# The rest of each w_down weight: a negated rounding on ScalarE and an adding DMA inside SBUF in place of a subtraction on VectorE

## The chip, the cores and the metric

The kernel runs on one core of a Trainium2 chip. The metric is the time of one execution on the device in microseconds, the median of several runs. One execution was also recorded by the hardware profiler, and all rows below are from that one.

## The reference

Two transformer blocks over 256 tokens of width 2048, in float32. The change lies in the feed-forward part of the first block, whose hidden width is 5632:

```python
h2 = rms_norm(x, norm2_g[l])
x = x + (jax.nn.silu(h2 @ w_gate[l]) * (h2 @ w_up[l])) @ w_down[l]
```

Before it stand the first block's two attentions (`w_in`, `w_out`), after it the second block's even and odd layers. Nearly all the work is products of a [256 x K] activation with a [K x N] weight that is read once from HBM.

## The kernel before

A float32 product is made of three products in float32r, a form with a shorter mantissa. Each operand v is split in `hi`, v rounded to float32r, and `lo`, the rest v - hi, also in float32r. TensorE then makes activation hi by weight hi, activation hi by weight lo, and activation lo by weight hi (L186, L187, L188).

`linear` (L168) does one product for 512 output columns. It walks over groups of 512 rows of the weight. For each group SP fetches one tile `raw` [128, 4, 512] (1 MB, L124) from HBM; three such tiles exist. A group is two pairs of row blocks. For each pair, `split` (L153) makes `hi` [128, 2, 512] by a cast on ScalarE (L155) and `lo` by a subtraction on VectorE (L156); three `hi` and three `lo` tiles exist. TensorE then runs twelve products on the pair: two row blocks, two tiles of 128 tokens, three products each. The results gather in two PSUM tiles `acc`.

The feed-forward part (L507 to L539) loops over 11 blocks `j` of 512 hidden columns: `linear` on `w_gate` (4 groups), `linear` on `w_up` (4 groups), the gate, a transposition to `mh` and `ml`. After j = 2, 4, 6, 8 it calls `down` on two blocks and after j = 10 on three. `down` does four `linear` on `w_down`, one per 512 output columns, each over two (at the end three) groups. So `w_down` is read in four stretches of 8 groups and a last one of 12: 44 groups, 88 pairs. They are called stages here. In the last one each column block is finished by `x_done` (transposes and splits of the new stream, sums of squares).

The order on each engine is set by a scheduler when the program is built, each engine runs its instructions in that order, and each waits on semaphores for what it reads and for the tile that it writes to be free. SP's fetch of a group waits until the tile of three groups before has been read by the last of its readers.

The tiles called `u` are the work tiles of the attentions (`unit`, L102); of these 0, 1, 2, 3, 6, 7, 8 and 11 are free during the feed-forward part.

Of the kernel before, what the change touches and what calls it, by code (L numbers as in the profile page):

```python
# [18 lines left out]
P = 128  # L19
# [5 lines left out]

# constants that depend on shapes alone, by column of one [128, *] array
CU, CR, CIND, CID, CMASK, COMASK, CGE, CLE, CGT, COROPE, CEND = 0, 128, 256, 258, 386, 514, 642, 770, 898, 1026, 1282


def _constants():  # L30
    c = np.zeros((P, CEND), np.float32)
    s, t = np.arange(P)[:, None], np.arange(P)[None, :]
    same = (s // 64) == (t // 64)
    c[:, CU:CU + P] = (same & (s <= t)) / 16.0
    c[:, CR:CR + P] = (same & (s > t)) / 16.0
    c[:, CIND:CIND + 2] = (np.arange(P)[:, None] // 64 == np.arange(2)[None, :]) / 16.0
    c[:, CID:CID + P] = s == t
    c[:, CMASK:CMASK + P] = same & (s <= t)
    c[:, COMASK:COMASK + P] = np.where(s >= t, 0.0, NEG)
    c[:, CGE:CGE + P] = s >= t  # L40
    c[:, CLE:CLE + P] = s <= t
    c[:, CGT:CGT + P] = s > t

    def angles(d):
        f = np.float32
        inv = f(1.0) / (f(10000.0) ** (np.arange(0, d, 2, dtype=f) / f(d)))
        ang = np.arange(S, dtype=f)[:, None] * inv[None, :]
        cos, sin = np.cos(ang).astype(f), np.sin(ang).astype(f)
        return cos.reshape(2, P, d // 2).transpose(1, 0, 2), sin.reshape(2, P, d // 2).transpose(1, 0, 2)

    co, so = angles(64)
    c[:, COROPE:COROPE + 128] = np.concatenate([co, co], 2).reshape(P, 128)
    c[:, COROPE + 128:COROPE + 256] = np.concatenate([-so, so], 2).reshape(P, 128)

    # even layer: rope tables and the decay of the retention, keys on partitions
    ce, se = angles(256)
    gam = np.zeros((P, 4, S), np.float64)
    diff = np.arange(S)[None, :] - np.arange(P)[:, None]
    for h in range(4):
        gam[:, h] = np.where(diff >= 0, (1.0 - 2.0 ** (-5.0 - h)) ** np.maximum(diff, 0), 0.0)  # L60
    ev = np.concatenate([ce.reshape(P, 256), se.reshape(P, 256), gam.reshape(P, 1024)], 1).astype(np.float32)

    # relative bias: bucket of each distance, and the log of how many patterns hold it
    x = np.arange(384)
    d = 255 - x
    dd = np.clip(d, 0, None)
    big = 16 + (np.log(np.maximum(dd, 1) / 16) / np.log(2048 / 16) * 16).astype(np.int64)
    bucket = np.where(dd < 16, dd, np.minimum(big, 31))
    oneh = (bucket[None, :] == np.arange(32)[:, None]).astype(np.float32)
    cnt = (d >= 0) * ((d <= 128) * 1 + (d % 4 == 0) * 1 + (d % 16 == 0) * 1)  # L70
    lnc = np.where(cnt > 0, np.log(np.maximum(cnt, 1)), NEG).astype(np.float32)
    rel = np.zeros((32, 768), np.float32)
    rel[:, :384] = oneh
    rel[:, 384:] = lnc[None, :]
    return {"c_main": c, "c_even": ev, "c_rel": rel}
# [3 lines left out]
def model(ctx, tc, a, out):  # L79
# [31 lines left out]

# [1 line left out]
    cm = cst.tile([P, CEND], F32, tag="cm", name="cm")  # L113
# [37 lines left out]

# [1 line left out]
    def split(hi, lo, src, scale=None):  # L153
# [10 lines left out]

    # small products of an attention, dealt out among the large ones
    side = deque()

    def linear(w, c0, n, groups, got=(), fine=False):  # L168
        accs = [ps_acc.tile([P, 512], F32, tag="acc", name=nm("acc")) for _ in range(2)]
        for gi, ((xh, xl), kg) in enumerate(groups):  # L170
            raw = got[gi] if gi < len(got) else fetch(w, kg, c0, n)
            for k in range(4):
                k2 = k % 2
                if k2 == 0:
                    hi = hl_p.tile([P, 2, 512], F32R, tag="hi", name=nm("hi"))
                    lo = hl_p.tile([P, 2, 512], F32R, tag="lo", name=nm("lo"))
                    if fine and gi == 0:
                        for j in range(2):
                            split(hi[:, j, :n], lo[:, j, :n], raw[:, k + j, :n])
                    else:  # L180
                        split(hi[:, :, :n], lo[:, :, :n], raw[:, k:k + 2, :n])
                for t in range(2):
                    o = accs[t][:, :n]
                    st, en = gi == 0 and k == 0, gi == len(groups) - 1 and k == 3
                    sl = slice(t * P, (t + 1) * P)
                    T.matmul(o, xh[:, k, sl], hi[:, k2, :n], start=st, stop=False)  # L186
                    T.matmul(o, xh[:, k, sl], lo[:, k2, :n], start=False, stop=False)  # L187
                    T.matmul(o, xl[:, k, sl], hi[:, k2, :n], start=False, stop=en)  # L188
                    if side:
                        side.popleft()()  # L190
        return accs

# [1 line left out]
    def new_stream():  # L194
# [40 lines left out]
    def head_scale(accs_t, nh, r, r2, t):  # L235
        """per token and head: r * (r^2 * mean of squares + eps)^-0.5"""
        dh = 512 // nh
# [11 lines left out]
    def finish_head(po, gate, g_off, rowf, chunk, mixT, scales):  # L249
        """o [tok, 256] of one head in po [128, 2, 256]: RMS over it, the gate, transposed and split"""  # L250
        s, q = small([2], "fs"), small([2], "fq")
# [22 lines left out]
    def silu_gate(dst, acc, rh_t):  # L274
        """(1 + tanh(z/2)) * acc, z = 2 rh acc: silu(z) is this by rh"""
        A.activation(dst, acc, AF.Tanh, scale=rh_t)  # L276
        V.scalar_tensor_tensor(dst, dst, 1.0, acc, ALU.add, ALU.mult)  # L277

    def transpose_rows(src, dst, scale=None):
        """src(t) [128 tok, 4 x 128] -> dst [128, 4, 256]"""  # L280
        for j in range(2):
# [10 lines left out]

    # ================= first block: mixers =================
    st = new_stream()
# [12 lines left out]

    # r and the gate's low rank part
    got = first
# [79 lines left out]

    # relative bias of the dilated heads by distance  # L390
    relr = sm.tile([P, 384], F32, tag="Lx", name="relr", bufs=4)
    pt = ps_w.tile([P, 512], F32, tag="w", name=nm("at"))
    T.matmul(pt[:8, :384], rb[0:32, :], rel[0:32, 0:384], start=True, stop=True)
    V.tensor_tensor(relr[:8, :], pt[:8, :384], rel[0:8, 384:768], ALU.add)
    # laid down once a row; a row pitch read one short turns it into a Toeplitz table
    reld = dr.tile([8, 384], F32, name="reld", tag="reld")
# [47 lines left out]

    # dilated attention: the three patterns are one softmax, a distance counted as often as patterns hold it
    Tb = []
# [59 lines left out]

    # ================= first block: feed forward =================  # L507
    w_gate, w_up, w_down = a["w_gate"][0], a["w_up"][0], a["w_down"][0]
# [6 lines left out]
    def down(bs, last):  # L515
        for b in range(4):
            x_add(b, linear(w_down, b * 512, 512, [(acts[j], j) for j in bs]))
            if last:
# [23 lines left out]

    # ================= second block, even layer =================
    ev_w_in, ev_w_out = a["ev_w_in_2"][0], a["ev_w_out_2"][0]
# [58 lines left out]

    # gated convolution, half a width at a time; channels on partitions for the taps
    rc = small([2], "rc")
# [48 lines left out]

    # ================= second block, odd layer =================
    od_w_in, od_w_out = a["od_w_in_2"][0], a["od_w_out_2"][0]
    mixT = [pair(mt_p, "m") for _ in range(4)]
    # rope tables with the norm weights in them: x * ra + swapped(x) * rb
    ra = cst.tile([P, 2, 2, 64], F32, tag="ra", name="ra")
# [9 lines left out]
    def rope_odd(dst, acc, nh, w, t, scale):  # L669
        """acc [128, nh*64] -> dst, roped and scaled per head"""  # L670
        n = nh * 64
# [15 lines left out]
    for t in range(2):  # L687
        q = head_scale(accs[t], 8, r, r2, t)
        rope_odd(krow[:, t], accs[t], 4, 1, t, q)
        A.activation(vo[:, t], accs[t][:, 256:], AF.Copy, scale=r[:, t:t + 1])  # L690
    # keys of a group twice, the dead half zero: a pair of query heads in one product
    kz = [unit(2 + i, [2, 2, S], F32R) for i in range(2)]
# [23 lines left out]
    def att_scores(c):  # L716
        """queries of a tile against their 128 keys: of tile 1 the keys past a query's own place are the first
        tile's, so one square holds the whole window"""
        g, t, u = c["g"], c["t"], c["u"]
# [60 lines left out]
    def att_values(c):  # L780
        """values still, probabilities moving: two heads side by side, transposed as the output product wants them"""
        g, t, u = c["g"], c["t"], c["u"]
# [105 lines left out]
```

## Time and profile before

| | |
|---|---|
| Median of three runs | 1939.45 us (1939.33 to 1939.72) |
| Span of the profiled execution | 1937.7 us |
| What the median has beyond that span | 1.75 us |
| TensorE busy in the span | 1925.6 us, 99% |
| VectorE, ScalarE, GpSimd busy | 1090.8, 900.2, 193.5 us |
| Moved by the DMA engines | 356.16 MB, mean 184 GB/s |

Engines are named PE (TensorE's products), PEld (its weight loads), DVE (VectorE), ACT (ScalarE), POOL (GpSimd), SP (the queue that fetches). A name with q behind it (SPq, POOLq) is the engine's sequencer. Busy time counts records of instructions. Records of products overlap by some 0.16 us (one is 0.39 us long and they start every 0.23 us), so a busy PE says that it never ran dry, not that it is at its peak. The DMA share is the mean over the 16 DMA engines of the time that their packets took; packets overlap, so it can pass 1.

### The profile page before, as it was taken

What the parts mean: (1) busy time and instruction counts of PE and PEld (TensorE: products, weight loads), DVE (VectorE), ACT (ScalarE), POOL (GpSimd) and SP (SyncE); (2) the same over time, 40 slices, a digit from 0 to 9 for tenths busy, and PEclk for the clock granted to TensorE, in tenths of its full rate; (3) what the DMA queues carried; (4) which work ended last, traced back from release to release, by engine and by line L of the source; (5) the groups of instructions that cost most, each with busy time, mean ns of one, the idle gap of its engine ahead of it and who ended that gap; (6) DMA issues with size and microseconds to landing.
All of it is one profiled execution on the core that took longest, in us unless ns stands there. A gap on an engine that the chain in (4) does not pass through costs nothing.

```text
span 1937.7 us, 22600 instructions
## 1 busy us (share of the span) xinstructions
PE 1925.6 (99%) x8928; PEld 1591.1 (82%) x8928; DVE 1090.8 (56%) x1287; ACT 900.2 (46%) x1239; POOL 193.5 (10%) x314
## 2 busy tenths in 40 slices
PE   8999999999999999999999999999999999999999
PEld 8877888888888888888888888888888888788787
DVE  5445555565555555555555555555555666677654
ACT  6544544454444434434444544444444355566543
POOL 2000221100000000000000001010000003754100
PEclk9999999999999999999999999999999999999999
DMA  8564555555555555555555555555556555443364
GB/s 286 194 211 157 178 183 171 190 175 193 182 190 196 195 186 185 194 195 191 184 192 194 187 183 178 172 189 169 186 192 196 184 185 193 159 143 137 131 206 141
DMA packets 181050, 356.16 MB, mean 184 GB/s; under 512 B 6072, under 2 KB 14288, under 8 KB 180816
## 3 DMA queue, kind: packets, MB, share of 16 engines
q1 hardware_dynamic: 179888, 351.03, 54.4%
q0 software_dynamic: 912, 3.64, 0.7%
q8 instruction: 70, 1.15, 0.2%
q14 instruction: 36, 0.29, 0.0%
q10 hardware_dynamic: 144, 0.05, 0.0%
HBM read 352.59 MB, written 3.68 MB: 184 GB/s over the span
## 4 chain that ended last, share of the span: by engine, by line
PE 98%; POOL 1%; DVE 0%; DMA 0%; ACT 0%; SPq 0%; issue 0%; ACTq 0%
PE acc L186 30%; PE acc L187 30%; PE acc L188 30%; PE at L787 1%; PE tr L204 1%; PE tr L286 1%; PE tr L535 0%; PE tr L768 0%; DMA xT<-in_x_t_dram 0%; PE at L735 0%; PE at L737 0%; PE at L736 0%; PE at L592 0%; PE at L441 0%; PE at L436 0%; PE at L429 0%
## 5 line engine op out<-in xcount | busy, mean ns | idle before, releaser
L156 DVE TENSOR_TENSOR lo<-raw,hi 128x1024 fp32r<-128x1024 f32 (+3 forms) x666 | 816.1, 1227 | 721.0 <-ACT hi L155 719.4
L155 ACT CAST hi<-raw 128x1024 fp32r<-128x1024 f32 (+3 forms) x666 | 692.4, 1040 | 865.6 <-PE acc L188 854.5
L187 PE MATMUL acc<-lo,xh 128*128 128x512 f32 (+3 forms) x1920 | 748.7, 390 | 0.4 <-DVE lo L156 0.4
L188 PE MATMUL acc<-hi,xl 128*128 128x512 f32 (+3 forms) x1920 | 742.9, 387 | 0.0
L186 PE MATMUL acc<-hi,xh 128*128 128x512 f32 (+3 forms) x1920 | 685.4, 389 | 6.3 <-ACT hi L155 6.3
L186 PEld LDWEIGHTS acc<-hi,xh 128*128 128x128 f32 x1920 | 359.9, 188 | 80.4 <-ACT hi L155 6.7
L187 PEld LDWEIGHTS acc<-lo,xh 128*128 128x128 f32 x1920 | 361.1, 188 | 72.5 <-issue 1.7
L188 PEld LDWEIGHTS acc<-hi,xl 128*128 128x128 f32 x1920 | 361.2, 188 | 71.3 <-issue 2.1
L187 PE MATMUL acc<-lo,mh 128*128 128x512 f32 x736 | 288.4, 392 | 0.0
L188 PE MATMUL acc<-hi,ml 128*128 128x512 f32 x736 | 286.7, 390 | 0.0
L186 PE MATMUL acc<-hi,mh 128*128 128x512 f32 x736 | 264.9, 392 | 0.0
L188 PEld LDWEIGHTS acc<-hi,ml 128*128 128x128 f32 x736 | 138.2, 188 | 28.1
L187 PEld LDWEIGHTS acc<-lo,mh 128*128 128x128 f32 x736 | 138.2, 188 | 28.1
L186 PEld LDWEIGHTS acc<-hi,mh 128*128 128x128 f32 x736 | 137.8, 188 | 28.2
L219 POOL TENSOR_SCALAR st_s<-st_s 128x2 f32<-128x2 f32 x4 | 0.8, 192 | 985.9 <-DVE st_s L218 985.9
L233 DVE TENSOR_TENSOR x<-x,acc 128x512 f32<-128x512 f32 x80 | 51.3, 680 | 5.6 <-PE acc L188 5.6
L276 ACT ACTIVATE u<-acc,st_rh 128x512 f32<-128x512 f32 (+3 forms) x46 | 29.2, 653 | 17.5 <-PE acc L188 16.7
L277 DVE SCALAR_TENSOR_TENSOR u<-u,acc 128x512 f32<-128x512 f32 (+3 forms) x46 | 28.8, 639 | 9.5 <-ACT u L276 9.5
L158 ACT ACTIVATE xh<-tr,gc 128x256 fp32r<-128x256 f32 x48 | 20.1, 471 | 20.7 <-PE tr L204 19.8
L755 ACT ACTIVATE Lx<-Lx,omx 128x128 f32<-128x128 f32 x64 | 24.9, 392 | 8.8 <-POOL omx L752 7.4
L159 DVE SCALAR_TENSOR_TENSOR xl<-tr,gc,xh 128x256 fp32r<-128x256 f32 x48 | 21.0, 478 | 11.5 <-ACT xh L158 11.5
L150 POOL TENSOR_TENSOR hq<-hs,nhalf 128x8 f32<-128x8 f32 (+1 forms) x18 | 25.9, 1438 | 0.8
(202 smaller groups left out, 854.1 us busy)
## 6 DMA issues: line engine op xcount, KB each, us to landing
raw<-in_ev_w_in_dram SPq DMA_DIRECT2D x64, 1024.0 KB, 5.1
raw<-in_w_gate_dram SPq DMA_DIRECT2D x44, 1024.0 KB, 4.9
raw<-in_w_up_dram SPq DMA_DIRECT2D x44, 1024.0 KB, 4.9
raw<-in_w_down_dram SPq DMA_DIRECT2D x44, 1024.0 KB, 4.9
raw<-in_w_in_dram SPq DMA_DIRECT2D x40, 1024.0 KB, 5.0
raw<-in_od_w_in_dram SPq DMA_DIRECT2D x36, 1024.0 KB, 4.8
raw<-in_w_out_dram SPq DMA_DIRECT2D x16, 1024.0 KB, 4.9
raw<-in_ev_w_out_dram SPq DMA_DIRECT2D x16, 1024.0 KB, 4.9
```

Source lines behind the costliest of these rows:

```text
L150: G.tensor_tensor(o, ms, nhalf[:, :ms.shape[-1]], ALU.pow)
L155: A.copy(hi, src)
L156: V.tensor_tensor(lo, src, hi.bitcast(F32), ALU.subtract)
L158: A.activation(hi, src, AF.Copy, scale=scale)
L159: V.scalar_tensor_tensor(lo, src, scale, hi.bitcast(F32), ALU.mult, ALU.subtract)
L186: T.matmul(o, xh[:, k, sl], hi[:, k2, :n], start=st, stop=False)
L187: T.matmul(o, xh[:, k, sl], lo[:, k2, :n], start=False, stop=False)
L188: T.matmul(o, xl[:, k, sl], hi[:, k2, :n], start=False, stop=en)
L233: V.tensor_tensor(xs, xs, accs[t], ALU.add)
L276: A.activation(dst, acc, AF.Tanh, scale=rh_t)
L277: V.scalar_tensor_tensor(dst, dst, 1.0, acc, ALU.add, ALU.mult)
L755: A.activation(L4[:, e], L4[:, e], AF.Exp, bias=mx[:, h:h + 1], accum_out=sx[:, h:h + 1])
```

## The change

For `w_down` alone, `lo` is no longer made on VectorE. ScalarE writes the negated rounding of the raw weight into one of eight `u` tiles, and GpSimd's queue issues a DMA that reads the raw weight in SBUF and adds it to that tile: lo = -round(raw) + raw. The cast of `hi` stays on ScalarE. The diff also drops comments, which moves line numbers behind L162 by up to 12.

```diff
-    def linear(w, c0, n, groups, got=(), fine=False):
+    los = [0]
+    def linear(w, c0, n, groups, got=(), fine=False, by_dma=()):
...
                 if k2 == 0:
                     hi = hl_p.tile([P, 2, 512], F32R, tag="hi", name=nm("hi"))
-                    lo = hl_p.tile([P, 2, 512], F32R, tag="lo", name=nm("lo"))
-                    if fine and gi == 0:
+                    if by_dma:
+                        lo = unit(by_dma[los[0] % len(by_dma)], [2, 512], F32R)
+                        los[0] += 1
+                        A.copy(hi, raw[:, k:k + 2])
+                        A.activation(lo, raw[:, k:k + 2], AF.Copy, scale=-1.0)
+                        G.dma_start(lo, raw[:, k:k + 2], accum_op=ALU.add)
+                    else:
+                        lo = hl_p.tile([P, 2, 512], F32R, tag="lo", name=nm("lo"))
+                    if by_dma:
+                        pass
+                    elif fine and gi == 0:
...
     def down(bs, last):
         for b in range(4):
-            x_add(b, linear(w_down, b * 512, 512, [(acts[j], j) for j in bs]))
+            x_add(b, linear(w_down, b * 512, 512, [(acts[j], j) for j in bs], by_dma=(0, 1, 2, 3, 6, 7, 8, 11)))
```

On ScalarE, where the first stage begins: `raw_4165` is the last group of `w_up`, `raw_4219` and those behind it are groups of `w_down`, and `u_778_4222` is the first `lo` in a work tile.

```order
 L155 CAST hi_4133<-raw_4131 128x1024
 L155 CAST hi_4149<-raw_4131 128x1024
+L183 ACTIVATE u_778_4222<-raw_4219 128x1024
+L183 ACTIVATE u_780_4239<-raw_4219 128x1024
 L155 CAST hi_4167<-raw_4165 128x1024
 L155 CAST hi_4183<-raw_4165 128x1024
-L155 CAST hi_4221<-raw_4219 128x1024
-L155 CAST hi_4237<-raw_4219 128x1024
-L155 CAST hi_4255<-raw_4253 128x1024
-L155 CAST hi_4271<-raw_4253 128x1024
+L183 ACTIVATE u_783_4258<-raw_4255 128x1024
+L183 ACTIVATE u_785_4275<-raw_4255 128x1024
```

The negated roundings of a group stand ahead of casts that belong to earlier pairs, so ScalarE makes them some two to three pairs before the `hi` of the same group, and a cast behind them waits until their group has landed.

On GpSimd, at the same place in the program, with the semaphores that each instruction waits for (`DMASW` and `DMAHW` are those of DMAs issued by GpSimd and by SP):

```order
 L522 TENSOR_SCALAR r2h_3317<-st_r_3315 128x2 [waits Pool_49]
+L184 DMA u_778_4222<-raw_4219 128x1024 [waits DMAHW4_49,Activation_49]
+L184 DMA u_780_4239<-raw_4219 128x1024 [waits Activation_49]
+L184 DMA u_783_4258<-raw_4255 128x1024 [waits DMAHW5_49,Activation_49]
+L184 DMA u_785_4275<-raw_4255 128x1024 [waits PE_49,Activation_49]
+L184 DMA u_790_4298<-raw_4295 128x1024 [waits DMAHW6_49,Activation_49]
+L184 DMA u_792_4315<-raw_4295 128x1024 [waits Activation_49]
+L184 DMA u_795_4334<-raw_4331 128x1024 [waits DMAHW7_49,DMASW3_49,Activation_49]
+L184 DMA u_797_4351<-raw_4331 128x1024 [waits DMASW4_49,Activation_49]
```

GpSimd's queue now holds the adding DMAs of all stages one behind the other, 88 of them, with no other instruction between the first and the last.

On SP, the fetches of the first five groups of that stage, now:

```order
L124 DMA raw_4219<-in_w_down_dram 128x4x512 [waits DMAHW1_49,DVE_49]
L124 DMA raw_4255<-in_w_down_dram 128x4x512 [waits DMAHW2_49,DVE_49]
L124 DMA raw_4295<-in_w_down_dram 128x4x512 [waits DMAHW3_49,DVE_49]
L124 DMA raw_4331<-in_w_down_dram 128x4x512 [waits DMASW6_49,DMAHW4_49,DMASW5_49,Activation_49]
L124 DMA raw_4371<-in_w_down_dram 128x4x512 [waits DMASW7_49,DMAHW5_49,DMASW0_49,Activation_49]
```

From the fourth group on a fetch waits for the two adding DMAs of the group three before it and for ScalarE, where it waited for VectorE.

## Rows read from the trace of the kernel before

**Rows 1.** The page: span, and busy time of each engine over it.
```profile
span 1937.7 us, 22600 instructions
...
PE 1925.6 (99%) x8928; PEld 1591.1 (82%) x8928; DVE 1090.8 (56%) x1287; ACT 900.2 (46%) x1239; POOL 193.5 (10%) x314
```

**Rows 2.** The page: chain of work that ended last, share by engine.
```profile
PE 98%; POOL 1%; DVE 0%; DMA 0%; ACT 0%; SPq 0%; issue 0%; ACTq 0%
```

**Rows 3.** Windows: first stage, last stage, then three stretches at the start.
```profile
core 0: us, PE busy (x) PEld busy (x) DVE busy (x) ACT busy (x) POOL busy (x), PEclk, DMA share, GB/s
541.49:585.94 44.45, 44.45 (x202) 36.85 (x200) 25.80 (x27) 17.85 (x18) 0.00 (x0) 1.00 0.57 189
1071.14:1140.13 68.99, 68.99 (x321) 57.30 (x320) 40.59 (x47) 34.90 (x50) 0.00 (x0) 1.00 0.55 183
2.00:12.00 10.00, 6.07 (x24) 5.60 (x24) 5.74 (x13) 6.60 (x15) 1.39 (x5) 1.00 0.97 319
12.00:22.00 10.00, 9.21 (x49) 8.88 (x50) 8.96 (x15) 7.77 (x14) 0.00 (x0) 1.00 1.06 399
22.00:32.00 10.00, 10.00 (x58) 10.00 (x58) 4.45 (x5) 6.67 (x13) 0.00 (x0) 1.00 1.04 389
```

**Rows 4.** Timeline of PE: first two pairs of the first stage, its end.
```profile
541.49 0.62 PE L186 MATMUL acc<-hi,mh 128*128 128x512 f32 x2
...
544.21 0.62 PE L186 MATMUL acc<-hi,mh 128*128 128x512 f32 x2
...
585.94 0.39 PE L186 MATMUL acc<-hi,xh 128*128 128x512 f32 x1
```

**Rows 5.** Timeline of PE: where the last stage begins and what follows it.
```profile
1071.14 0.62 PE L186 MATMUL acc<-hi,mh 128*128 128x512 f32 x2
...
1140.13 0.39 PE L186 MATMUL acc<-hi,xh 128*128 128x512 f32 x1
```

**Rows 6.** Groups by line in the first stage, 541.49 to 585.94: the lo subtraction.
```profile
L156 DVE TENSOR_TENSOR lo<-raw,hi 128x1024 fp32r<-128x1024 f32 x16 | 19.6, 1225 | 17.5 <-ACT hi L155 17.4
```

**Rows 7.** Groups by line on ACT in the last stage, 1071.14 to 1140.13.
```profile
L155 ACT CAST hi<-raw 128x1024 fp32r<-128x1024 f32 x24 | 25.3, 1055 | 26.9 <-PE acc L188 26.9
```

**Rows 8.** Timeline of SP: fetches of the first stage and of the last.
```profile
524.99 39.38 SPq L124 DMA_DIRECT2D raw<-in_w_down_dram  x8
...
1054.64 62.99 SPq L124 DMA_DIRECT2D raw<-in_w_down_dram  x12
```

**Rows 9.** Waits of SP's queue: engine, line, waited for: us, times, longest.
```profile
SPq L124 <- DVE lo L156: 1678.3, 317, 10.0
```

**Rows 10.** DMA issues: tile, queue, count, KB each, median us from issue to landing.
```profile
raw<-in_w_down_dram SPq DMA_DIRECT2D x44, 1024.0 KB, 4.9
...
u<-skew POOLq DMA_DIRECT2D x2, 512.0 KB, 4.1
```

**Rows 11.** Line L449, issues of u<-skew: ns min/median/max on POOL.
```profile
L449 POOL DMA_DIRECT2D u<-skew x2: 827/840/852, 162.8 to 196.1; - x2
```

**Rows 12.** DMA queues in 12 to 32 us, fetches alone.
```profile
DMA packets 4886, 7.88 MB, mean 394 GB/s; under 512 B 200, under 2 KB 3856, under 8 KB 4885
```

**Rows 13.** DMA queues in 108 to 125 us: MB and share of 16 engines.
```profile
q1 hardware_dynamic: 1100, 2.19, 38.3%
q0 software_dynamic: 176, 1.59, 33.0%
```

## The prediction

> **What bounds the kernel now.** I began with busy times and the chain of work. TensorE is busy for 1925.6 of 1937.7 us [rows 1] and makes 98% of the chain that ended last [rows 2]; VectorE, which the change relieves, has 0% of it. All the time in which TensorE ran dry is 12.1 us over the whole span, so no edit on another engine can win more than that. Then I read the stages by windows: in the first and in the last w_down stage PE is busy for 44.45 of 44.45 and 68.99 of 68.99 us, at the full granted clock, 1.00, which is the 2.4 GHz level [rows 3]. Nothing at all is to be won there. Last I read what stands behind TensorE. One pair takes it 544.21 - 541.49 = 2.72 us [rows 4], a group 5.44 us. In that time ScalarE works 1.06 us per pair and then waits for TensorE to free a `hi` tile [rows 7]; VectorE works 1.23 us and then waits for ScalarE [rows 6]; SP waits for VectorE before most fetches, 1678.3 us in all [rows 9]. Everything stands in line behind TensorE. The DMA engines move 189 GB/s in the first stage [rows 3], one fetch of 1.049 MB per 5.44 us. They are the resource to watch, for the change puts a second load on them.
>
> **What it takes away and what it adds.** Per pair it takes 1.225 us off VectorE, 88 x 1.225 = 108 us in all [rows 6]. VectorE is not on the chain, so this is worth 0. It adds three things.
>
> *ScalarE* gets 88 negated roundings of [128 x 1024]. The cast of the same shape takes 1.055 us [rows 7]; I take that, and 2.11 us per pair are still under 2.72. In the last stage ScalarE goes from 34.90 to 34.90 + 24 x 1.055 = 60.2 of 68.99 us [rows 3]. It costs nothing; the cover is gone if one negation takes over 34.09 / 24 = 1.42 us.
>
> *GpSimd's queue* issues 88 DMAs. An issue of the 512 KB transfer `u<-skew` kept POOL for 0.84 us [rows 11], and GpSimd does nothing else in the stages (0.00 us busy, [rows 3]). One issue per 2.72 us: hidden.
>
> *The DMA engines* get 88 transfers of 0.524 MB that add. The trace has no adding DMA and none from SBUF to SBUF, so I bound the price by rows. The engines moved 394 GB/s when fetches alone kept them full from 12 to 32 us [rows 12]. At that rate one fetch of a group costs 1.049 / 0.394 = 2.66 us of all engines, and a plain copy of a pair's 0.524 MB costs 1.33 us. That copy price is the lower bound. An add in place must read the raw weight and also the tile it adds to, so it reads twice what a copy reads: 2.66 us. For an upper bound I take the rate of the stage itself: 189 GB/s at a share of 0.57 are 332 GB/s for full engines [rows 3], 3.16 us per fetch and 3.16 us per doubled add. The nearest transfer that GpSimd's queue issued, 1.59 MB at 33.0% of 17 us, ran at 283 GB/s [rows 13], or 1.85 us per plain 0.524 MB, between the two. I take 2.66 us, since two reads belong to the operation whatever the rate.
>
> The Trainium skill has a price for this, in "Collectives: The Full Stack", section "The bandwidth ceiling: the fold count and why AG ≠ RS ≠ AR": an adding transfer emits two read descriptors per chunk on the same ring where a copy emits one, and a reduce-scatter was measured at 1.93 times less than an all-gather. Applied to the copy price it would be 1.93 x 1.33 = 2.57 us per add, an estimate from that page, and some 8 us less in the total; no row before shows an add.
>
> **The sum.** Per group the DMA engines then need 2.66 + 2 x 2.66 = 7.98 us where TensorE needs 5.44, so in the stages they become the bound. A stage does not lose all of 2.54 us per group, because its first fetch goes out before TensorE gets there: at 525.0, against 541.5 [rows 4, 8]. I balance the stage from that fetch to the landing of the last add. The work is 8 fetches, two fetches of the next stretch (their tiles are freed by earlier groups and they share the engines), and 16 adds: 10 x 2.66 + 16 x 2.66 = 69.2 us. To it come some 2.7 us in which the engines have nothing to add yet (landing 4.9 [rows 10], negation 1.06 and issue 0.84, 6.8 in all, less the first fetch's 2.66 and 1.4 of the second), and a tail of 4.1 - 0.84 - 1.33 = 1.9 us from the end of a transfer to its landing [rows 10, 11]. The last add lands at 525.0 + 73.8 = 598.8. TensorE wants it for its last pair at 585.9 - 2.7 = 583.2 [rows 4]. That is 15.6 us of stall, and four such stages make 62.4. The last stage has 14 fetches and 24 adds, 37.2 + 63.8 + 4.6 = 105.6 us from 1054.6 [rows 8], so 1160.2, against 1140.1 - 2.7 = 1137.4 [rows 5]: 22.8 us. Together 85.2 us. The span goes from 1937.7 to 2022.9; with the 1.75 us that the median has beyond the span, **2025 us**. Behind a stage nothing more is lost: the next fetches have already shared the engines, and w_gate has no adds.
>
> The same balance at the other prices: a plain copy price (1.33) ends at 525.0 + 52.5 = 577.5, 5.7 us before it is wanted, so 0. At 283 GB/s for the add alone (1.85) it is 2.6 us per stage and 3.4 in the last, 14 in all. With 3.16 for both it is 82.2 + 4.6 = 86.8, less 58.2, so 28.6 per stage and 120.1 + 4.6 - 82.8 = 41.9 at the end, 156 in all. An add begins to cost at (58.2 - 31.2) / 16 = 1.69 us.
>
> **The rivals.** (0.2%, or 3.9 us, is about what a measurement of this kernel can tell from no change.)
>
> *A, the add is hidden (not slower).* If the read of the destination runs beside the other read, an add costs 1.33 us and a group 5.32 of 5.44 us. The eight work tiles speak for it: `lo` is made two to three pairs ahead, so latency alone is covered. Against it is how little is spare, 0.12 us per group. Time 1939.5, or up to 1953 at 1.85 us.
>
> *B, the new wait at the raw tile.* A fetch now waits for both adds of three groups before. Unshared, the loop is 4.9 landing + 3 x 1.06 on ScalarE + 0.84 issue + 1.33 (the second add queues behind the first) + 3.26 landing = 13.5 of the 16.3 us that three groups take, 2.8 spare. If shared transfers stretch it to twice their length (2.66 + 2.66 more) the loop is 18.8, 0.8 us per group, 44 x 0.8 = 37, less the lead of 8 x 2.54 - 15.6 = 4.7 us per stage: 14 us, 1953. It needs transfers that collide each time though the engines are not full; it decides from 2.8 us of stretch per loop.
>
> *C, an add is far slower than two reads* (a slow adder in the path). At twice my price, 5.32 us, a stage needs 26.6 + 85.1 + 4.6 = 116.3 less 58.2, so 58.1, and the last 169.5 - 82.8 = 86.7: 319 us, 2259. No row speaks for it or against it.
>
> *D, the clock falls.* With holes in TensorE's work the granted clock could drop to the 1.2 GHz level in the stages; a pair would take 5.44 us, the adds would be hidden, and the stages cost 4 x 44.45 + 69 = 247 more: 2186. Against it: from 2 to 12 us PE was busy for 6.07 of 10 us and the granted clock stayed 1.00 [rows 3]; in the stages it would be busy for 5.44 of 7.98. The Trainium skill ("TensorE: Matmul & The Clock Gate", "Part 1: The HAM clock gate (the "warmup" mystery)") has the clock follow how busy the array has been; by it short holes are harmless, and that row agrees.
>
> *E, faster.* Only the 12.1 us of dry time could go (1927 at the most), and none of it is in the stages.
>
> **Chances.** My forecast, DMA-bound stages with doubled reads, 55%, 1993 to 2095 by itself (adds of 2.3 us, or 9.8 us per stage and 14.2 in the last, to 3.16 us). A 21%, of which 4 in its upper part; B 6%; C 12%; D 2%; E 4%. So slower by over 0.2% is 55 + 4 + 6 + 12 + 2 = 79%, within 0.2% 17%, faster 4%. The range must take in A, so it goes from 1936 to 2095; it leaves out E, C and D.
>
> **What would show it.** In the stages: DMA share near 1 and about 3 MB moved or read per 8 us; L187 (lo) waiting for the adding DMA; a group at about 8 us; the w_down fetches landing later than 4.9 us; adds landing 5 us or more after issue; VectorE's lo count down by 88; no change outside the stages. I am wrong if an add takes under 1.7 us of the engines (then nothing moves), if ScalarE's negation takes over 1.42 us (then ScalarE binds the last stage), or if SP's queue waits while the DMA engines are idle (then B).

## The result and the profile after

| | before | after |
|---|---|---|
| Median on the same chip | 1939.39 us (1939.27 to 1939.72) | 2023.77 us (2019.77 to 2025.49) |
| Span of the profiled execution | 1937.7 us | 2021.4 us |

The ratio is 1.0432, with an interval of 1.042 to 1.0445. The kernel became 84.4 us slower; 2025 us were forecast.

The page of the changed kernel, span and busy time, then the chain of work that ended last, by engine and by line:

```profile
span 2021.4 us, 22874 instructions
...
PE 1954.1 (97%) x8928; PEld 1598.6 (79%) x8928; DVE 987.2 (49%) x1199; ACT 977.6 (48%) x1327; POOL 266.2 (13%) x402
...
PE 81%; DMA 14%; ACT 2%; issue 1%; POOL 1%; DVE 1%; SPq 0%; POOLq 0%; ACTq 0%
PE acc L199 25%; PE acc L200 25%; PE acc L198 25%; DMA raw<-in_w_down_dram 9%; DMA u<-raw 5%; ACT hi L182 1%; ACT u L183 1%; PE at L799 1%; PE tr L298 1%; PE tr L216 0%; POOL u L184 0%; PE tr L780 0%; DVE lo L156 0%; PE tr L547 0%; DMA xT<-in_x_t_dram 0%
```

Against [rows 1, 2]: DMA, which had 0% of the chain, has 14%, and both halves of it belong to w_down, its fetches 9% and its adds 5%. VectorE has its 88 instructions less (1199 against 1287) and ScalarE its 88 more (1327 against 1239). TensorE's dry time, span less busy, went from 12.1 to 67.3 us. That is 55.2 of the 83.7 us by which the span grew. The other 28.5 us are in PE's busy time, for the same 8928 products; where they come from is said behind the timeline of TensorE.

The windows of the five w_down stages, from the first product on a w_down pair to the last (columns as in [rows 3]):

```profile
541.30:604.19 62.89, 51.50 (x201) 40.08 (x200) 9.05 (x13) 28.38 (x30) 10.18 (x12) 0.89 1.00 254
692.16:750.41 58.25, 49.56 (x202) 38.51 (x201) 7.75 (x12) 28.40 (x30) 10.17 (x12) 0.94 1.03 265
838.38:896.05 57.67, 49.02 (x202) 37.32 (x201) 9.21 (x13) 28.41 (x30) 10.18 (x12) 0.97 1.04 267
984.02:1046.36 62.34, 48.72 (x202) 37.32 (x200) 7.34 (x11) 28.18 (x30) 10.23 (x12) 0.97 0.98 249
1134.32:1223.88 89.56, 76.48 (x322) 59.01 (x321) 14.76 (x25) 52.10 (x70) 16.95 (x20) 0.94 1.04 266
```

Before, the first four lasted 44.45 us each and the last 68.99 ([rows 3] shows the first and the last). They are longer by 18.4, 13.8, 13.2, 17.9 and 20.6 us, 83.9 in all: the whole loss is inside the stages. The DMA share of the first stage went from 0.57 to 1.00 (0.98 to 1.04 in the others), and the granted clock, 1.00 before, is under 1 in every stage.

What TensorE, ScalarE and SP's queue waited for, over the whole span (us, times, longest):

```profile
PE acc L198 <- ACT hi L182: 31.5, 12, 4.6
PE acc L199 <- DMA u<-raw: 23.7, 28, 3.4
...
ACT u L183 <- DMA raw<-in_w_down_dram: 139.4, 40, 9.4
...
SPq L124 <- DMA u<-raw: 310.0, 55, 9.5
SPq L124 <- ACT hi L182: 14.7, 12, 3.1
```

The two waits of TensorE add up to the 55.2 us of new dry time. Only the smaller one is for the add. The larger is for the cast of `hi`, which the change leaves on ScalarE as it was and only moves in its order. To see why, follow the chain through the first stage (start, length, what):

```profile
535.68 13.54 DMA raw<-in_w_down_dram
549.36 0.86 issue
550.21 1.04 ACT u L183
551.25 1.89 ACT hi L182 x2
...
575.11 15.14 DMA raw<-in_w_down_dram
```

And ScalarE's timeline there (start, length, in brackets how long it had been idle and for what):

```profile
549.25 2.00 ACT L183 ACTIVATE u<-raw 128x1024 fp32r<-128x1024 f32 x2 [9.42 <-DMA raw<-in_w_down_dram]
551.16 1.97 ACT L182 CAST hi<-raw 128x1024 fp32r<-128x1024 f32 x2
...
590.33 2.00 ACT L183 ACTIVATE u<-raw 128x1024 fp32r<-128x1024 f32 x2 [8.64 <-DMA raw<-in_w_down_dram]
592.24 2.92 ACT L182 CAST hi<-raw 128x1024 fp32r<-128x1024 f32 x3
```

A fetch of w_down took 13.5 us. ScalarE stood 9.4 us at the negation of that group, and the cast that TensorE needed next, of a group already landed, stood behind it in the queue. Then TensorE's own timeline at that place:

```profile
547.42 0.40 PE L200 MATMUL acc<-hi,ml 128*128 128x512 f32 x1
552.24 0.80 PE L198 MATMUL acc<-hi,mh 128*128 128x512 f32 x1 [4.42 <-ACT hi L182]
552.84 0.63 PE L199 MATMUL acc<-u,mh 128*128 128x512 f32 x1
553.26 0.63 PE L200 MATMUL acc<-hi,ml 128*128 128x512 f32 x1
...
557.91 0.39 PE L199 MATMUL acc<-u,mh 128*128 128x512 f32 x1
558.14 0.39 PE L200 MATMUL acc<-hi,ml 128*128 128x512 f32 x1
```

TensorE was dry for 4.42 us, and behind that hole products start every 0.43 us, the 1.2 GHz level; at 558 they are back at 0.23. A second hole, of 3.54 us up to 593.3, has the same sequel.

Only part of the 28.5 us of longer busy time is the clock. By the granted clock of the five windows it is some 19 us at most (62.89 x 0.11 + 58.25 x 0.06 + 57.67 x 0.03 + 62.34 x 0.03 + 89.56 x 0.06). The rest, some 9 us or more, fits the edges of TensorE's 12 + 28 = 40 new holes: at each the 0.16 us by which records overlap counts anew, and the first product behind it takes longer (0.50 us at 587.22, behind a hole of 0.88 us, where others take 0.39).

Last, the transfers: issues with the median us to landing, over the whole span; then the queues from 525 to 605 us (packets, MB, share of 16 engines), q0 the adds, q1 the fetches:

```profile
raw<-in_w_down_dram SPq DMA_DIRECT2D x44, 1024.0 KB, 9.8
u<-raw POOLq DMA_DIRECT2D x88, 512.0 KB, 8.9
```
```profile
q0 software_dynamic: 2304, 8.39, 55.5%
q1 hardware_dynamic: 5788, 11.52, 40.1%
```

The sixteen adds took 55.5% of 80 us, 2.78 us of all engines each; a fetch of 1.049 MB took 2.92 us. A w_down fetch lands in 9.8 us (median; the longest took 16.2) where it took 4.9 [rows 10].

### The profile page after: what moved, and what is told of

The parts are those of the page before. It is cut to its first block, busy times and chain, and to the rows that moved or that the text cites. A ratio compares the mean times of both kernels' runs of the same rounds, so it can differ in the third digit from the quotient of the medians.

```text
span 2021.4 us, 22874 instructions
## 1 busy us (share of the span) xinstructions
PE 1954.1 (97%) x8928; PEld 1598.6 (79%) x8928; DVE 987.2 (49%) x1199; ACT 977.6 (48%) x1327; POOL 266.2 (13%) x402
## 4 chain that ended last, share of the span: by engine, by line
PE 81%; DMA 14%; ACT 2%; issue 1%; POOL 1%; DVE 1%; SPq 0%; POOLq 0%; ACTq 0%
PE acc L199 25%; PE acc L200 25%; PE acc L198 25%; DMA raw<-in_w_down_dram 9%; DMA u<-raw 5%; ACT hi L182 1%; ACT u L183 1%; PE at L799 1%; PE tr L298 1%; PE tr L216 0%; POOL u L184 0%; PE tr L780 0%; DVE lo L156 0%; PE tr L547 0%; DMA xT<-in_x_t_dram 0%
## 5 line engine op out<-in xcount | busy, mean ns | idle before, releaser
L156 DVE TENSOR_TENSOR lo<-raw,hi 128x1024 fp32r<-128x1024 f32 (+3 forms) x578 | 708.9, 1229 | 670.4 <-ACT hi L155 667.4
L155 ACT CAST hi<-raw 128x1024 fp32r<-128x1024 f32 (+3 forms) x578 | 599.0, 1038 | 735.4 <-PE acc L200 705.6
L199 PE MATMUL acc<-lo,xh 128*128 128x512 f32 (+3 forms) x1920 | 748.6, 390 | 0.4 <-DVE lo L156 0.4
L200 PE MATMUL acc<-hi,xl 128*128 128x512 f32 (+3 forms) x1920 | 742.9, 387 | 0.0
L198 PEld LDWEIGHTS acc<-hi,xh 128*128 128x128 f32 x1920 | 359.9, 188 | 80.3 <-ACT hi L155 6.5
L199 PEld LDWEIGHTS acc<-lo,xh 128*128 128x128 f32 x1920 | 361.1, 188 | 72.4 <-issue 1.7
L200 PEld LDWEIGHTS acc<-hi,xl 128*128 128x128 f32 x1920 | 361.2, 188 | 71.3 <-issue 2.1
L198 PE MATMUL acc<-hi,mh 128*128 128x512 f32 x736 | 280.6, 403 | 31.6 <-ACT hi L182 31.5
L200 PE MATMUL acc<-hi,ml 128*128 128x512 f32 x736 | 293.5, 399 | 0.0
L184 POOL DMA_DIRECT2D u<-raw x88 | 74.9, 855 | 722.5 <-ACT u L183 693.3
L199 PE MATMUL acc<-u,mh 128*128 128x512 f32 x352 | 146.5, 416 | 23.8 <-DMA u<-raw 23.7
L200 PEld LDWEIGHTS acc<-hi,ml 128*128 128x128 f32 x736 | 141.7, 193 | 28.8
L183 ACT ACTIVATE u<-raw 128x1024 fp32r<-128x1024 f32 x88 | 88.2, 1050 | 139.4 <-DMA raw<-in_w_down_dram 139.4
L199 PE MATMUL acc<-lo,mh 128*128 128x512 f32 x384 | 150.8, 393 | 0.0
L199 PEld LDWEIGHTS acc<-u,mh 128*128 128x128 f32 x352 | 70.0, 199 | 50.1 <-DMA u<-raw 36.5
L182 ACT CAST hi<-raw 128x1024 fp32r<-128x1024 f32 x88 | 88.4, 1040 | 11.4 <-PE acc L200 11.3
L199 PEld LDWEIGHTS acc<-lo,mh 128*128 128x128 f32 x384 | 72.1, 188 | 14.6
L156 DVE TENSOR_TENSOR ml<-tr,mh 128x512 fp32r<-128x512 f32 x26 | 17.4, 688 | 73.2 <-ACT mh L155 73.2
```

The source lines that it names most:

```text
L155: A.copy(hi, src)
L156: V.tensor_tensor(lo, src, hi.bitcast(F32), ALU.subtract)
L182: A.copy(hi, raw[:, k:k + 2])
L183: A.activation(lo, raw[:, k:k + 2], AF.Copy, scale=-1.0)
L184: G.dma_start(lo, raw[:, k:k + 2], accum_op=ALU.add)
```

## The experiments

The expectations number the theories. Theory 1 is the forecast's: an add costs the DMA engines two reads, they are full in the stages, and that alone sets the time. Theory 4 came out of the profile after: the cast stuck behind a negation makes the loss. The other numbers are rivals that the expectations describe: ScalarE's added work and new order, the wait at the raw tile, and the turns that packets take on the DMA engines.

| run | median, us | ratio to before, interval |
|---|---|---|
| e1 add on VectorE | 1940.17 | 1.0003, 0.9994 to 1.0013 |
| e2 plain copy | 1945.23 | 1.0033, 1.0022 to 1.0043 |
| e7 copies and adds alone | 2003.69 (one run) | not taken |
| e3 44 adds | 1941.79 | 1.0018, 1.0008 to 1.0028 |
| e12 68 adds | 2008.94 | 1.0355, 1.0335 to 1.0375 |
| e13 176 adds | 2226.54 | 1.1484, 1.1465 to 1.1504 |
| e4 adds halved in size | 2025.78 | 1.044, 1.0423 to 1.0458 |
| e5 fourth raw tile | 2024.9 | 1.0441, 1.0425 to 1.0458 |
| e8 cast ahead of negation | 2134.92 | 1.1008, 1.0991 to 1.1024 |
| e11 negation on GpSimd | 2056.75 | 1.0609, 1.0592 to 1.0627 |
| e9 changed kernel, more products | 2090.55 | 1.0776, 1.076 to 1.0792 |
| e10 kernel before, more products | 1999.3 | 1.0307, 1.0292 to 1.0323 |

### The add on VectorE, all else as changed

```diff
-                        G.dma_start(lo, raw[:, k:k + 2], accum_op=ALU.add)
+                        V.tensor_tensor(lo, raw[:, k:k + 2], lo.bitcast(F32), ALU.add)
```

> The negated rounding stays on ScalarE, in nearly the changed kernel's order and into the eight work tiles, but VectorE makes the sum in place of the 88 adding DMAs. Theory 1 (the DMA engines are full in the stages because an add costs them twice a copy): all of the loss goes, 1939 to 1943 us. Rival 2 (ScalarE's 88 extra roundings and the moved order, with casts queued behind roundings that wait for their group): most of the loss stays, 1990 us or more. Rival 3 (the fetch that waits for the adds): nearly all goes too, this run does not tell it from theory 1.

The time is that of before, 1.0003. Its first stage:

```profile
541.57:586.02 44.45, 44.45 (x201) 36.83 (x200) 22.84 (x25) 28.70 (x30) 0.00 (x0) 1.00 0.56 188
```

The 88 negations are all still there, most of them in the changed kernel's order ahead of casts, and cost nothing while fetches land in 5.0 us. The loss comes with the adding DMAs. As expected, this run does not tell the engines' load from the fetch that waits for the adds.

### A plain copy in place of the add

```diff
-                        G.dma_start(lo, raw[:, k:k + 2], accum_op=ALU.add)
+                        G.dma_start(lo, raw[:, k:k + 2])
```

> The 88 DMAs stay, in the same queue and with the same waits, but copy the raw weight over the work tile and do not add (so lo is the whole weight; the subtraction is left out). Theory 1: a copy costs the engines 1.3 to 1.5 us in place of 2.8, a group 2.9 + 2.8 = 5.7 us of the 5.44 that TensorE needs, so little or nothing is lost behind the lead: 1939 to 1955 us. Rival 3 (the chain of waits from fetch to rounding to issue to landing, with the engines not the limit): all these waits are still there, and only the transfer is shorter by some 1.4 us in a chain of 16.3 us: 1990 us or more.

It is 1.0033, some 6 us. Transfers, bytes, packets and the order of ScalarE are those of the changed kernel; the adding is gone, and GpSimd's issue takes 0.53 us in place of 0.85. Rival 3 had 1990 us or more and is out as the whole cause. First stage, and queues from 525 to 587 us:

```profile
541.43:586.13 44.70, 44.70 (x202) 36.78 (x201) 9.05 (x13) 28.56 (x30) 6.36 (x12) 1.00 0.98 337
```
```profile
q1 hardware_dynamic: 5794, 11.52, 54.0%
q0 software_dynamic: 2304, 8.39, 39.0%
```

A copy takes 39.0% of 62 us over 16, 1.51 us, and a fetch by the same count 3.05. The engines are at a share of 0.98, and TensorE does not run dry in this stage. A group takes 3.05 + 2 x 1.51 = 6.07 us of the engines, 0.63 more than TensorE's 5.44, and the head start of the first fetch takes up most of that: by the forecast's balance a stage needs 10 x 3.05 + 16 x 1.51 + 4.6 = 59.3 us of 58.2, the last 83.5 of 82.8, which makes 5 us in all. So a share near 1 is no loss by itself; the doubled price of the add is what no longer fits. That this price is a second read is not seen in a row: the queue counts 2304 packets and 8.39 MB for the adds and for the copies alike.

### The price alone

Sixteen copies and sixteen adds of 0.524 MB inside SBUF, at the end of the kernel before, with nothing beside them:

```diff
...
+    for i in range(16):
+        G.dma_start(dst[i % 8], src)
+    for i in range(16):
+        G.dma_start(dst[i % 8], src, accum_op=ALU.add)
...
```

> The kernel before, with 16 copies of 0.524 MB from SBUF to SBUF and then 16 adding DMAs of the same tile put behind its last outputs, all from GpSimd's queue and with nothing beside them. Theory 1: a copy takes 1.3 to 1.5 us of the 16 engines and an add 2.6 to 2.8 us, at equal bytes written. Against it: equal times of copy and add (then the loss is not the doubled read), or an add of over 4 us (then it is a slow adder).

GpSimd's timeline, where each issue waits for an earlier transfer, so that their starts show its pace (L859 copies, L861 adds):

```profile
1944.18 0.54 POOL L859 DMA_DIRECT2D u<-u  x1 [0.89 <-DMA u<-u]
...
1948.14 0.54 POOL L859 DMA_DIRECT2D u<-u  x1 [0.76 <-DMA u<-u]
...
1966.66 0.85 POOL L861 DMA_DIRECT2D u<-u  x1 [1.67 <-DMA u<-u]
...
1979.35 0.84 POOL L861 DMA_DIRECT2D u<-u  x1 [1.67 <-DMA u<-u]
```

Three copies take 3.96 us, 1.32 each. Five adds take 12.69 us, 2.54 each, 1.92 times a copy. The run took 2003.69 us; 16 x (1.32 + 2.54) = 61.8 of the 64.3 us more.

### The dose: 44, 68 and 176 adds

Only the first pair of each group by DMA; all but the second pair of each odd group; and every add twice, the second into a spare tile that nothing reads (two of the eight work tiles are the spare ones, six are left for `lo`):

```diff
-                    if by_dma:
+                    if by_dma and k == 0:
```
```diff
-                    if by_dma:
+                    dma_lo = by_dma and not (gi % 2 and k)
+                    if dma_lo:
```
```diff
                         G.dma_start(lo, raw[:, k:k + 2], accum_op=ALU.add)
+                        G.dma_start(spare[los[0] % 2], raw[:, k:k + 2], accum_op=ALU.add)
```

> Only the first pair of each group is made by the adding DMA, 44 in all; the second pair is split as before with VectorE. Theory 1: 2.9 + 2.8 = 5.7 us of engine time per group against 5.44, so at most 0.3 us per group less the lead: 1939 to 1950 us, less than a quarter of the loss. Rival 3: the fetch still waits for an adding DMA in each group and the chain is as long: half of the loss or more stays, 1980 us or more.

> The adding DMA makes lo for 68 of the 88 pairs (three of four in the first four stages, five of six in the last), VectorE for the rest. Theory 1, by the balance of a stage with the prices that the runs have shown: at 2.66 per fetch and 2.54 per add (each alone) 3.5 us per stage and 9.8 in the last, 24 us; at the shares in the changed kernel's stage (2.92 and 2.78) 9 and 18, 54 us: 1964 to 1995 us. If the loss went with the number of adds, 68 of 88 would cost 65 us or more: 2004 or more.

> Behind each add a second one of the same size into one of two spare tiles that nobody reads (six work tiles are left for lo), 176 adds in all. Theory 1: the balance with 32 adds per stage of 8 groups gives 27 + 81 + 4.6 - 58.2 = 54 to 29 + 89 + 4.6 - 58.2 = 65 us per stage and 81 to 96 in the last, 297 to 356 us: 2237 to 2300 us, and up to 40 more for TensorE's slow clock and the waits at two spare tiles. If an add's cost lay in what waits for it and not in the engines, the second add, for which nothing on TensorE waits, would cost little: under 2080 us.

The forecast's balance (2.66 us per transfer, 4.6 us of lead and tail, 58.2 and 82.8 us to spend) gives 0 for 44 adds, 85 for 88, 319 for 176. Measured were 2.3, 84.4 and 287. With 44 adds rival 3 (1980 us or more) is out; with 176 the time is 10 us under theory 1's range and far over its rival's 2080. For 68 adds the forecast's balance gives 4 x 4.9 + 12.2 = 32, and 69.6 was measured: there it is wrong by a factor of two, and the time lies over theory 1's range (1995) and in that of a loss that goes with the number of adds (2004 or more). That rule does not hold either: it would give 42 us at 44 adds. First stage with 68 adds, and TensorE's waits over the span (L199 reads `hi` in this run, L200 `lo`):

```profile
541.27:597.33 56.06, 49.65 (x202) 39.77 (x200) 13.88 (x17) 25.66 (x27) 7.63 (x9) 0.91 0.95 254
```
```profile
PE acc L199 <- ACT hi L183: 41.5, 16, 5.9
...
PE acc L200 <- DMA u<-raw: 5.4, 6, 2.6
```

The add is hardly waited for. Nearly all dry time ends with a cast, behind a fetch that came late, and the clock falls here too. The median fetch of w_down lands in 8.0 us, as with copies (7.9), but the longest takes 14.3 us (11.1 with copies), and ScalarE stands at negations for fetches 130.8 us (67.9 with copies, 139.4 in the changed kernel). The balance of a stage does not see that; what would remove it was not found.

### Packets of half the size

```diff
-                        G.dma_start(lo, raw[:, k:k + 2], accum_op=ALU.add)
+                        for j in range(2):
+                            G.dma_start(lo[:, j], raw[:, k + j], accum_op=ALU.add)
```

> The changed kernel, each adding DMA cut in two of 128 x 512, so 176 of them, with packets of 2 KB in place of 4 KB; a fetch has packets of 2 KB. The engines took the two queues in turn packet by packet, it seems: a fetch that shared with adds took 13.5 us, which is one add packet (4 KB, read twice) for each packet of its own. Then with smaller add packets a w_down fetch should land in some 7 us in place of 9.8, the adds later. Theory 1: the work of the engines is the same, so the time moves little, 2005 to 2030 us. If the late fetch is the cause of the loss and not the full engines: below 1985.

Nothing moved: 2025.78 us, a w_down fetch lands in 9.5 us (9.8 before this edit). With adds of 2 KB packets, as the fetches have, the fetch is as late as with 4 KB, so it isn't an unequal turn between large and small packets that delays it. Some 7 us had been expected. Since the fetch did not get earlier, the run does not test what an earlier fetch would bring.

### A fourth raw tile

```diff
-    raw_p = ctx.enter_context(tc.tile_pool(name="raw_p", bufs=3))
+    raw_p = ctx.enter_context(tc.tile_pool(name="raw_p", bufs=4))
...
-                        lo = hl_p.tile([P, 2, 512], F32R, tag="lo", name=nm("lo"))
+                        lo = hl_p.tile([P, 2, 512], F32R, tag="lo", name=nm("lo"), bufs=2)
```

The space comes from VectorE's `lo` tiles and two kinds of work tile elsewhere (`Lx`, `junk2`), one fewer of each.

> The changed kernel with a fourth raw tile (and to make room two lo tiles of VectorE's in place of three, three Lx and two junk2 tiles, which may cost some us outside of the stages; so the stages are read by themselves, 83.9 us lost in the five). Theory 1: the engines have the same work, the first fetch of a stage goes out one group earlier and one fetch more of the next stretch shares, 2.7 to 5 us won per stage: 55 to 75 us lost in the stages. Rival 3 (the fetch waits for the adds of three groups before): most of the loss goes, under 35 us in the stages.

Same time, 2024.9. SP's queue:

```profile
SPq L124 <- ACT hi L182: 182.9, 36, 10.2
SPq L124 <- DMA u<-raw: 120.4, 30, 9.3
```

The five stages lose 80.3 us; theory 1 had 55 to 75, rival 3 under 35. SP's wait for adds fell from 310.0 to 120.4 us, but its wait for casts, which also free the tile, rose from 14.7 to 182.9; together they went from 324.7 to 303.3. The fetches of the first stage went out 2 us earlier or more (the first at 522.6, not 524.8), and fetches landed later (11.8 us after issue, not 9.8). The stages stayed at a DMA share of 1.01 to 1.03. So the wait for the adds at the raw tile is not what sets the time; a kernel in which a fetch waits for no tile was not run.

### The cast ahead of the negation

```diff
-                        A.copy(hi, raw[:, k:k + 2])
-                        A.activation(lo, raw[:, k:k + 2], AF.Copy, scale=-1.0)
+                        tc.keep_in_program_order(A.copy(hi, raw[:, k:k + 2]))
+                        tc.keep_in_program_order(A.activation(lo, raw[:, k:k + 2], AF.Copy, scale=-1.0))
```

> The changed kernel with ScalarE held to the order in which the code is written: cast of a pair, then its negated rounding, so no cast stands behind a rounding of a later group; but each lo then begins two to three pairs later. Theory 1 (full engines, whatever the order): the five stages lose as much or a little more, 80 to 120 us of the 83.9, with the DMA share at 0.95 or more; the holes are spread over the pairs, so the granted clock stays at 1.00. Theory 4 (a cast stuck behind a rounding that waits for its fetch makes the holes): under 50 us in the stages.

The worst of the variants with 88 adds, 2134.92. TensorE's waits:

```profile
PE acc L199 <- DMA u<-raw: 118.3, 44, 7.5
PE acc L198 <- ACT hi L182: 11.5, 8, 1.8
```

The wait for the cast did shrink, from 31.5 to 11.5. But a negation behind its own cast, which waits for TensorE to free a `hi` tile, loses the lead of two to three pairs, and each add's way to its landing lies open: 118.3 us for 23.7. From 541 to 601 us the DMA share is 0.87, so the engines have gaps, and the granted clock is 0.80, where 1.00 was expected. Theory 4 (under 50 us) is not borne out; the lead that the scheduler's order gives is worth more than the stuck casts cost. Theory 1 (80 to 120 us) was far too low here as well, against a loss of 195 us: it counts on that lead. The run changes two things at once, so it does not say what the stuck casts cost.

### The negation on GpSimd

```diff
-                        A.activation(lo, raw[:, k:k + 2], AF.Copy, scale=-1.0)
-                        G.dma_start(lo, raw[:, k:k + 2], accum_op=ALU.add)
+                        tc.keep_in_program_order(G.tensor_scalar(lo, raw[:, k:k + 2], -1.0, None, ALU.mult))
+                        tc.keep_in_program_order(G.dma_start(lo, raw[:, k:k + 2], accum_op=ALU.add))
```

> The changed kernel with the negated rounding on GpSimd, in its queue just ahead of the add that needs it, so ScalarE has only the casts and none of them stands behind a rounding, while lo still runs ahead. A [128 x 1024] operation of GpSimd takes some 2.6 us (1.3 for 512 columns in the profile), with the issue 3.4 us per pair, 6.9 per group, less than the 8.1 to 8.4 us of the DMA engines. Theory 1: 60 to 100 us lost in the stages, DMA share near 1. Theory 4: under 45 us in the stages. If GpSimd becomes the bound the DMA share falls under 0.85.

Casts are free of negations here, their wait is 7.9 us, and the kernel is at 2056.75, 33 us behind the changed one. GpSimd's groups by line:

```profile
L183 POOL TENSOR_SCALAR u<-raw 128x1024 fp32r<-128x1024 f32 x88 | 267.4, 3039 | 474.4 <-DMA raw<-in_w_down_dram 474.4
L184 POOL DMA_DIRECT2D u<-raw x88 | 78.9, 897 | 26.9 <-POOL u L183 25.8 <-issue 1.0
```

With 3.04 + 0.90 us per pair GpSimd needs 7.9 us per group, nearly as much as the DMA engines (2.92 + 2 x 2.78 = 8.5), and the negation again starts only once its group has landed. In the first stage the DMA share is 1.00, so GpSimd is not the bound by the sign that was expected for it (under 0.85). Theory 1 had 60 to 100 us, theory 4 under 45; lost were 117. The run shows that casts out of the way do not bring the time back, not what they cost.

### More products beside the adds

Three more products per pair into a PSUM tile that nothing reads, in the changed kernel and in the one before. If the engines' load alone set the stage, TensorE would do them in its dry time.

```diff
+                if by_dma and k2 == 1:
+                    ex = ps_w.tile([P, 512], F32, tag="w", name=nm("ex"))
+                    for _ in range(3):
+                        T.matmul(ex, xh[:, k, :P], hi[:, 0], start=True, stop=True)
```

> The changed kernel, with three more products on TensorE per w_down pair (into a PSUM tile that nobody reads), 3 x 0.227 = 0.68 us per pair, 59.8 us in all. Theory 1 (the DMA engines set the pace of a stage, 8.4 us per group): TensorE needs 6.8 us per group with them, still less, so the products fill holes: 0 to 25 us over the 2024 of the changed kernel. Rival 3 (a chain of waits through TensorE, which frees the hi and lo tiles): the chain grows by the products, +50 to +60 us, 2075 or more.

> The control: the kernel before with the same three products per pair. Both theories: +60 us, 1999 us, for TensorE has no hole there.

In the kernel before they cost 59.5 us, their plain length. In the changed one they cost 66.8 us: nothing is hidden, where theory 1 had 0 to 25 us, and rival 3's forecast (2075 us or more) came true. TensorE's dry time did not shrink, it went from 67.3 to 82.1 us. A stretch of its first stage, then TensorE's and SP's waits:

```profile
580.00:590.00 10.00, 2.05 (x5) 1.66 (x6) 0.00 (x0) 4.83 (x5) 1.70 (x2) 0.65 0.62 132
```
```profile
PE acc L198 <- ACT hi L182: 70.9, 15, 9.9
...
SPq L124 <- DMA u<-raw: 195.8, 43, 7.4
SPq L124 <- ACT hi L182: 146.7, 32, 10.3
```

SP waits for the cast 146.7 us where it was 14.7, and for adds 195.8 us where it was 310.0; from 580 to 590 both TensorE (2.05 us busy) and the DMA engines (0.62) have gaps. Over whole stages the DMA share is 0.89 to 0.93 here, so the engines are no longer full. Read together: a fetch waits for the cast that frees its tile, the cast for TensorE to free a `hi` tile, and TensorE for a cast that stands behind a negation that waits for a fetch. Full engines would lengthen that loop, and what is added to TensorE would lengthen it too. The loop is a reading of these waits, no run opens it. What the run shows is that the engines' load does not set the pace alone.

## Where the prediction was right, and where not

*VectorE's relief is worth 0, ScalarE and GpSimd are hidden.* Right for their busy time. A negation took 1050 ns (1.055 us taken), an issue 855 ns (0.84). e1 has the negations for nothing; e2 has VectorE relieved, the negations and 88 issues, and is 6 us slower, not faster. Where the negations stand in ScalarE's order was not priced, and it did cost (below).

*Two reads per add, 2.66 us.* The price is right, the step on which the forecast rests: 2.54 us alone and 2.78 beside fetches, and at the price of a copy (e2) the loss is 6 of 84 us. That the price comes from a second read is the prediction's argument, and no row counts reads. The Trainium skill's factor ("Collectives: The Full Stack", "The bandwidth ceiling: the fold count and why AG ≠ RS ≠ AR"), 1.93 between an all-gather and a reduce-scatter, which adds, agrees with 1.92 here.

*The balance of a stage.* Right in size: 15.6 us forecast for each of four stages, 13.2 to 18.4 found; 22.8 for the last, 20.6 found. The last two adds of the first stage were issued by GpSimd from 591.7 us and took about 6.2 us, so the last landed at about 598 to 599; 598.8 was forecast. But TensorE did not wait for that add. It was dry for a cast until 593.3, and from there it ran the last three pairs without a hole, the first of them at the lower clock, to 604.2; the forecast had 601.5. So in this stage the size was met on another path than the one in the sum. Nothing was lost outside the stages, as said.

*How the loss looks.* Wrong. TensorE was to wait for the add, a little in each group. It waits 23.7 us for adds and 31.5 us for casts, in holes of up to 4.6 us. The new order of ScalarE (a cast behind a negation waits for that group's fetch) was shown ahead of the prediction, and the prediction expected fetches to land later; it did not put the two together, and its sum has no term for them.

*The clock (rival D, 2%).* The forecast kept 1.00 through the stages, and that step failed. Behind the second long hole of the first stage it was 0.66; the window of the changed kernel there:

```profile
590.00:600.00 10.00, 6.68 (x18) 5.30 (x19) 0.04 (x1) 5.88 (x6) 1.70 (x2) 0.66 0.86 196
```

The row on which the forecast rested, from 2 to 12 us [rows 3], had TensorE busy for 6.07 of 10 us at a granted clock of 1.00. The timeline of the kernel before reads otherwise there (products of 400 columns; start, length):

```profile
7.19 0.54 PE L187 MATMUL acc<-lo,xh 128*128 128x400 f32 x1
7.53 0.54 PE L188 MATMUL acc<-hi,xl 128*128 128x400 f32 x1
...
9.80 0.34 PE L187 MATMUL acc<-lo,xh 128*128 128x400 f32 x1
9.98 0.34 PE L188 MATMUL acc<-hi,xl 128*128 128x400 f32 x1
```

Behind the first 5.7 us of the span, in which TensorE had nothing to do, they start every 0.33 us until 8.9 us, and from 9.1 us on every 0.18. That is a factor of 1.9, as between 0.43 and 0.23 for the products of 512 columns above: they ran at the pace of the lower level, though the column says 1.00. So the row did not speak against rival D; if anything it spoke for it. The length of a hole alone does not tell when the clock falls: over the 3 us behind holes of 2.91 and 3.38 us (products from 1020.15 and 1034.04) it was 1.00 in the changed kernel, behind one of 2.16 us (737.67) 0.68. The Trainium skill describes a case like this one in "TensorE: Matmul & The Clock Gate", section "HAM oscillation — how this bites in real kernels", a kernel whose clock drops at its waits for DMA; the prediction cited another section of the page and took comfort from it. The fall costs some 19 us of slower products at most, not the 247 us of rival D, whose clock stayed low.

*So is 2025 against 2023.8 luck in part?* Yes. With the prices that the runs gave, the same balance makes 75 us (2.66 and 2.54, each alone) or 110 us (2.92 and 2.78, beside each other) of the 84, so the agreement to 1 us is luck, and the size is right to within a third. One piece of the lead in that sum, 1.4 us of the second fetch, comes from no row. Part of the slow products must lie in time that TensorE would have waited anyway, and how much was not separated. That the balance fits at 44 and 88 adds, is a tenth too high at 176 and half the loss at 68 (32 against 69.6), and that e9 hides nothing, shows that it isn't the whole rule. Shown is that the add's price, near twice a copy's, makes the loss (e1, e2, e7). Argued from rows only is the loop through late fetch, stuck cast and freed tile by which a stage loses it. Not tried was an order with casts ahead that keeps the negations' lead.

*The other rivals.* A (hidden) needs 1.69 us per add or less; e2, at 1.51, is what it would have looked like. B (the wait at the raw tile) is there, 310.0 us of SP's time; with most of the wait for adds gone the time is the same (e5), but the tile was still waited for, so what that wait costs stays open. C (an add far slower than two reads) is out by e7.

## What to carry to other kernels

Price a DMA that adds as two transfers, and set it against what the DMA engines have over in that very stage, not over the kernel: here 5.44 us per group less 2.9 for the fetch, room for about one add (2.5 to 2.8 us) and not for two, and 44 adds cost 2.3 us where 88 cost 84. Relieving an engine that has no part in the chain won nothing here, while the resource that took over the work lacked the room for it. When fetches become late, look for what stands behind the first instruction that waits for them on an engine's queue, and at the pace of TensorE's products behind its holes, not at the clock column alone.

## What the runs showed of the hardware that was not expected

- A fetch of 1 MB that shares the DMA engines with adds lands 9.8 us after its issue (median; 13.5 and 15.1 us for two of the first stage, 16.2 at most), though its own bytes take 2.9 us of the engines. With the adds' packets halved the median is 9.5 us.
- After holes of 3.5 and 4.4 us in the first stage TensorE ran at 1.2 GHz for some 5 us, products every 0.43 us. At the start of the kernel before the products show the same slow pace, while the clock column says 1.00.
- GpSimd's negation of [128 x 1024] takes 3.04 us, where ScalarE takes 1.05. Its issue of an adding DMA takes 0.85 us, that of a plain copy of the same size 0.54 (e7).
